# Early shares of an output projection: whole blocks at the heads' ends, or halves spread over more heads

## The chip, the core and the metric

The kernel runs on one core of a Trainium2 chip. The metric is the device time of one execution in microseconds. TensorE (PE in the profile, PEld for its weight loads) does the matmuls, VectorE (DVE), ScalarE (ACT) and GpSimd (POOL) the elementwise work; SyncE (SP) issues the DMA transfers. Each engine takes its instructions in order and waits on semaphores for the others. Matmul results land in PSUM, which the kernel divides into eight buffers of 512 columns.

## What is computed

One inference step of a two-layer decoder over 256 prompt tokens and 64 sample tokens (8 sequences of 8), T = 320 in all, model width 1024. Layer A is a chunked spatial-gating mixer with an FFN behind it; layer B is an mLSTM mixer with 8 heads and again an FFN. The change lies in layer B's mixer:

```
def mlstm_mixer(x, conv_buf, C0, n0, m0, w_in, conv_w, conv_b, b_i, b_f, gn_g, w_out):
    p = x @ w_in
    ...
    qk, new_buf = causal_dwconv(qk_pre, conv_buf, conv_w, conv_b)
    qk = jax.nn.silu(qk).astype(jnp.float32)
    ...
    h, C, n, m = mlstm_chunkwise(q, k, v32, ig, lf, ...)
    ...
    hn = ((h - mu) * lax.rsqrt(var + EPS)).reshape(bsz, s, D_B) * gn_g.astype(jnp.float32)
    o = jax.nn.sigmoid(o_pre.astype(jnp.float32))
    y = (o * hn).astype(x.dtype) @ w_out
    return y, new_buf, C, n, m
```

Each head gives 256 columns of `o * hn`, so the product with `w_out` sums over 8 heads × 256 = 2048 terms, which are 16 slices of 128, two a head. Its 1024 output columns are 8 output blocks of 128. The result is added to the residual stream `x`.

## The kernel before

**Arithmetic.** Everything is float32. A product of accuracy near float32 is made of three matmuls in a faster, rounded format: each operand is split into a high part (rounded) and a low part (the rest), and high × high, high × low and low × high are summed (three matmuls of 128 × 128 weights with 320 columns for each slice of 128). In layer B's mixer (`low_last`) a chunk first runs all matmuls with the weights' high part (the high sweep, two a slice), then all with the low part (the low sweep, one a slice).

**Weights.** `weights` (line 65) writes down the whole order in which weight chunks are used, as a list of (tensor, output block, first slice, slices). A chunk has up to 8 slices. `prefetch` (line 120) loads chunks in that order by SP into `raw` (4 buffers) and splits them: ACT casts the high part `wh` (line 154), DVE subtracts for the low part `wl` (line 155), 3 buffers each. `take` (line 165) hands over the next chunk, and has loads issued 4 chunks and splits 1 chunk ahead. `chunk` (line 173) issues a chunk's matmuls; `block` (line 185) takes a PSUM buffer from the pool `psm` (tag `pm`, 3 buffers) and sums as many chunks as its slices need. A second pool, `psa` (tag `pa`, 5 buffers), serves the smaller sums of the mixer.

**Order.** All matmuls keep the order of the program (`pin`, line 43), and the chunks' casts and subtractions keep theirs among each other. The other DVE and ACT work is put in order by a scheduler, so the program's text alone does not give it.

**A head of layer B** (loop in `layer_b`, from line 1055). For head h (from 1 on) the core runs, in this order on PE: the q block; parts of the state product of head h−1 (`inter`); the k block; the rest of `inter` and the sums of head h−1 (`numer`, tiles `num`); the first v block; the prompt's state (`state_prompt`, tile `pCp`) and a quarter of the samples' state (`state_sample`, tile `pcs`); the second v block; another quarter; `scores` (tiles `pMb`, `psc`); the first output-gate block; a quarter; the second gate block; `finish(h-1)`, which transposes the normalised rows `hn` (tiles `phn`), multiplies by the gate and splits the result into `yhb` and `ylb`, slices 2(h−1) and 2(h−1)+1 for the output projection; the last quarter; `k_nat` and `v_nat` (transposes into `pk`, `pv`, with DVE and ACT work that makes `kgs`, `kgh`, `kgl`, `vh`, `vl`, `vb`); and the first part of `inter` for head h. Six blocks of 8 slices a head are 144 large matmuls. The epilogues (`qk_epi`, `v_epi`, `o_epi`, `stats`) are DVE and ACT work beside that. In heads whose `state_sample` is wide (below h = 6) one of its two tiles comes from `psm`.

**Early output.** Once heads 0 to 3 are finished, their 8 slices can be multiplied with `w_out` before the remaining heads are done. `EARLY_OUT` (line 118) says where: the key (h, r) is a place in head h (r = 0 behind the q block, 1 behind `numer`, 2 ahead of the second v block, 3 behind `scores`, 4 ahead of the second gate block, 5 at the head's end), the value the output blocks whose share of slices 0 to 7 is made there. `early` (line 1015) runs the block and adds it to the residual stream by `residual` (line 301, one DVE add of 128 × 320 out of PSUM, tile `xT`). The other 8 slices follow in and behind head 7: `begin` (line 1048) starts output blocks 0 and 1 in head 7 and block 2 behind it and holds their `psm` buffers until the last heads' slices are added.

**The end of the mixer** (lines 1117 to 1150). Behind head 7 come `begin(0)`, `begin(1)`, the last `inter` and `numer`, the first gate block of head 7, `stats` with the first gate's epilogue in between, `state_prompt`, the second gate block with `o_epi` (line 1136), `finish(7)`, and the output blocks' second halves.

Of the kernel before, what the change touches and what calls it, by code (L numbers as in the profile page):

```python
# [10 lines left out]
F32 = mybir.dt.float32  # L11
# [5 lines left out]
P = 128  # L17
# [5 lines left out]
KD = D // P  # L23
# [14 lines left out]
class Net:  # L38
# [26 lines left out]
    def weights(self):  # L65

        I = self.I
        q = []

        def add(w, b, *groups, k0=0):  # L70
            for kn in groups:
                q.append((w, b, k0, kn))
                k0 += kn


        add(I["a_wv"], 0, 4)
        add(I["a_wv"], 4, 4)
        add(I["a_wv"], 0, 4, k0=4)
        for b in range(1, 4):
            add(I["a_wv"], b, 4, 4)  # L80
        add(I["a_wv"], 4, 4, k0=4)
        for b in range(5, 16):
            add(I["a_wv"], b, 8)
        for b in range(16):
            add(I["a_win"], b, 8)
        for b in range(KD):
            add(I["a_wo"], b, 8, 8)

        def ffn(l):
            for b in range(2 * KF):  # L90
                add(I["f_up"][l], b, 8)
            for b in range(KD):
                add(I["f_dn"][l], b, 8, 7, 7)

        ffn(0)
        add(I["b_wg"], 0, 8)
        for h in range(NH):
            for r in range(6):
                r = (0, 2, 1, 3, 4, 5)[r] if h == 0 else r
                if (h, r) == (NH - 1, 4):  # L100
                    for k0, n in ((8, 4), (12, 2)):
                        for b in (0, 1):
                            add(I["b_wo"], b, n, k0=k0)
                add(I["b_win"], 6 * h + r, 8)
                for b in self.EARLY_OUT.get((h, r), ()):
                    add(I["b_wo"], b, 8)
        add(I["b_wo"], 2, 6, k0=8)
        for b in (0, 1, 2):
            add(I["b_wo"], b, 2, k0=14)
        for b in range(3, KD):  # L110
            add(I["b_wo"], b, 8, k0=8)
        ffn(1)
        self.wq = q
        self.loaded, self.halved, self.used = [], [], 0

    AHEAD, SPLIT_AHEAD = 4, 1
    low_last = False
    EARLY_OUT = {(4, 5): (0, 1), (5, 3): (2,), (5, 5): (3, 4), (6, 3): (5,), (6, 5): (6, 7)}

    def prefetch(self, n, m):  # L120

# [60 lines left out]
                if sweep:  # L182
                    self.mm(ps[:, :T], wl[:, k, :], xh, False, last and k == kn - 1)

    def block(self, kt, rhs):

        ps = self.psm.tile([P, 512], F32, tag="pm", name="pm")
        done = 0
        while done < kt:
            kn = self.wq[self.used][3]  # L190
            self.chunk(ps, lambda k: rhs(done + k), done == 0, done + kn == kt)
            done += kn
        return ps
# [307 lines left out]
    def ffn(self, l, gnext):  # L501
# [3 lines left out]
        with tc.tile_pool(name=f"yf{l}", bufs=1) as yp, tc.tile_pool(name=f"lf{l}", bufs=1) as lp:  # L505
# [58 lines left out]
            else:  # L564
                self.final(lambda m: self.block(KF, rhs), lp)

    def final(self, block, lp):

        nc, O = self.nc, self.O
# [6 lines left out]
        for m in range(last):  # L576
            self.residual(m, block(m))
            self.square_block(m)
            gain(m)

        ps = block(last)
        x = self.xT[:, last, :]
        sq = self.tp.tile([P, T], F32, tag="sq", name="sq", bufs=2)
# [51 lines left out]
    def layer_b(self):  # L635
        nc, tc, I, O = self.nc, self.tc, self.I, self.O
# [4 lines left out]
        with ExitStack() as ctx:  # L641
# [109 lines left out]
            Y = {}  # L751
# [128 lines left out]
            def k_mask(h):  # L880
                _, _, kgs, kgz = S[h]["kg"]
                if h == NH - 1:
                    for b in range(NB):
                        nc.scalar.activation(kgz[:, b, :], kgs[:, b // 4, :].bitcast(F32), AF.Copy, scale=mk[:, b:b + 1])
                    return
                for i in (0, 4):
                    nc.gpsimd.tensor_tensor(kgz[:, i:i + 4, :], kgs[:, i // 4, :].bitcast(F32).unsqueeze(1).to_broadcast([P, 4, P]),
                                            mk[:, i:i + 4].unsqueeze(2).to_broadcast([P, 4, P]), op=MULT)
# [104 lines left out]
            def o_epi(h, j, ps):  # L993
                o = lp.tile([P, T], F32, tag="ob", name="o_b", bufs=1)
                nc.vector.tensor_tensor(o, ps[:, :T], self.rb, op=MULT)  # L995
                th = lp.tile([P, T], F32, tag="tho", name="th_o", bufs=4)
                nc.scalar.activation(th, o, AF.Tanh, scale=0.5)
                S[h].setdefault("o", []).append(th)

            def finish(h):  # L1000
                s = S[h]
                yh = hp.tile([P, 2, T], F32R, tag="yhb", name="yhb", bufs=6)
                yl = hp.tile([P, 2, T], F32R, tag="ylb", name="ylb", bufs=6)
                for e in range(2):
                    pt = self.psa.tile([P, 512], F32, tag="pa", name="phn")
                    for t in range(3):
                        self.tr(pt[:, t * P:(t + 1) * P], hn[:, t, e * P:(e + 1) * P], self.ident)
                    y = self.tp.tile([P, T], F32, tag="yf", name="y_b", bufs=2)
                    nc.vector.scalar_tensor_tensor(y, s["o"][e], 1.0, pt[:, :T], op0=ADD, op1=MULT)
                    g = gnh[:, 2 * h + e:2 * h + e + 1]  # L1010
                    nc.scalar.activation(yh[:, e, :], y, AF.Copy, scale=g)
                    nc.vector.scalar_tensor_tensor(yl[:, e, :], y, g, yh[:, e, :].bitcast(F32), op0=MULT, op1=SUB)
                    Y[2 * h + e] = (yh[:, e, :], yl[:, e, :])

            def early(h, r):
                for m in self.EARLY_OUT.get((h, r), ()):
                    self.residual(m, self.block(8, lambda k: Y[k]))

            with tc.tile_pool(name="rows", bufs=1) as rp:
                gates(rp)  # L1020
# [22 lines left out]
            def blk():  # L1043
                return self.block(KD, self.x_rhs)
# [12 lines left out]
            for h in range(NH):  # L1057
                if h:
                    qk_epi(h, 0, blk())
                    early(h, 0)  # L1060
                    if h == 1:
                        inter(0, 0)
                        state_split(0, 3)
                    inter(h - 1, 1)
                    qk_epi(h, 1, blk())
                    for i in (2, 3):
                        inter(h - 1, i)
                    numer(h - 1)
                    early(h, 1)
                    ps = blk()  # L1070
                    with self.behind_split():
                        stats(h - 1)
                    v_epi(h, 0, ps)
                    v_first(h - 1)
                    state_prompt(h - 1)
                    state_sample(h - 1, 0)
                    early(h, 2)
                    v_epi(h, 1, blk())
# [39 lines left out]
            h = NH - 1  # L1118
# [6 lines left out]
            ps = blk()  # L1125
# [7 lines left out]
            v_first(h)  # L1133
            state_prompt(h)
            k_mask(h)
            o_epi(h, 1, blk())
            finish(h)
            state_sample(h, 0)
            begin(2)
# [1 line left out]
            for m in range(KD):  # L1141
                ps = part.get(m)
                if ps is None:
                    ps = self.block(8, lambda k: Y[8 + k])
# [155 lines left out]
```

## Time and profile before

| | us |
|---|---|
| median of 3 runs | 955.85 |
| lowest and highest run | 955.83, 956.19 |
| the profiled execution | 956.05 |
| its span, first to last instruction | 954.3 |
| layer B's mixer, first block to last output matmul | about 424 to 712 |

The profile is of one execution. "PE L54 MATMUL pm<-xh,wh" is a matmul on PE from line 54, from the tiles xh and wh into pm; the buffer numbers are left out. Blocks on the layer's input read `xh` and `xl`, early output reads `yhb` and `ylb`. A matmul's length in a row is from start to landing; since matmuls overlap, the next one starts well before that, and the distance of two starts is what a matmul costs PE. Rows of the order in time give start, length, instruction, and in brackets the idle time ahead of it.

### The profile page before, as it was taken

The page shows a single profiled execution, that of the slowest core. Times are in us where ns is not written, and L with a number is a line of the kernel's source. Part 1 is how long each engine was busy: PE and PEld are TensorE (multiplying, and loading weights), DVE is VectorE, ACT ScalarE, POOL GpSimd, SP SyncE. Part 2 cuts the span into 40 slices and gives each one's busy share as a digit, 9 for nine tenths or more (in the row PEclk, how much of TensorE's full clock was granted, in tenths as well). Part 3 has the DMA queues.
Part 4 walks back from the last instruction along what each step waited for, and adds up shares of the span by engine and source line. Part 5 has one row for each costly group of instructions (what it writes and reads, how often), then busy time and mean ns, then how long its engine had stood idle before and what let it go on. Part 6 is the DMA issues. An engine that isn't in the chain of part 4 may idle for free.

```text
span 954.3 us, 17131 instructions
## 1 busy us (share of the span) xinstructions
PE 947.3 (99%) x6427; PEld 933.8 (98%) x6427; DVE 697.3 (73%) x1331; ACT 531.9 (56%) x978; POOL 115.8 (12%) x291
## 2 busy tenths in 40 slices
PE   9999999999999999999999999999999999999997
PEld 8889999999999999999999999999999999999997
DVE  6766976577777754559999998788897777775443
ACT  7557543454555443458777876666766445544342
POOL 2200000010000000014333322102102000000000
PEclk9999999999999999999999999999999999999999
DMA  8643346444444465565465655553474444445441
GB/s 270 210 153 133 133 137 198 160 146 147 149 156 155 139 183 147 149 216 175 128 212 175 206 178 196 185 183 118 132 247 148 149 145 154 156 144 155 143 141 56
DMA packets 54214, 155.19 MB, mean 163 GB/s; under 512 B 7372, under 2 KB 11980, under 8 KB 54132
## 3 DMA queue, kind: packets, MB, share of 16 engines
q1 hardware_dynamic: 54132, 154.10, 50.5%
q8 instruction: 51, 0.84, 0.4%
q14 instruction: 31, 0.25, 0.1%
HBM read 142.10 MB, written 11.97 MB: 161 GB/s over the span
## 4 chain that ended last, share of the span: by engine, by line
PE 94%; DVE 3%; ACT 1%; POOL 1%; DMA 0%; issue 0%; SPq 0%; POOLq 0%
PE pm L54 81%; PE pv_a L54 6%; PE num L54 2%; PE pmix L54 1%; PE pcs L54 1%; PE psc L54 1%; PE phn L57 0%; PE pCp L54 0%; DMA raw<-in_a_wv 0%; PE pv L57 0%; DVE wl L155 0%; PE pc L54 0%; DVE bcv L767 0%; PE pg L54 0%; PE pk L57 0%
## 5 line engine op out<-in xcount | busy, mean ns | idle before, releaser
L154 ACT CAST wh<-raw 128x1024 fp32r<-128x1024 f32 (+3 forms) x256 | 257.0, 1004 | 294.1 <-PE pm L54 161.7
L155 DVE TENSOR_TENSOR wl<-raw,wh 128x1024 fp32r<-128x1024 f32 (+3 forms) x256 | 299.0, 1169 | 118.9 <-ACT wh L154 115.0
L54 PE MATMUL pm<-xh,wh 128*128 128x320 f32 x1216 | 372.3, 311 | 0.1
L54 PE MATMUL pm<-xl,wh 128*128 128x320 f32 x1216 | 370.3, 309 | 0.0
L54 PE MATMUL pm<-xh,wl 128*128 128x320 f32 x1216 | 321.2, 309 | 0.0
L54 PEld LDWEIGHTS pm<-xh,wh 128*128 128x128 f32 x1216 | 228.4, 188 | 0.4 <-DVE o_b L995 0.3
L54 PEld LDWEIGHTS pm<-xl,wh 128*128 128x128 f32 x1216 | 228.4, 188 | 0.2
L54 PEld LDWEIGHTS pm<-xh,wl 128*128 128x128 f32 x1216 | 214.5, 188 | 0.0
L54 PE MATMUL pm<-yh_f,wh 128*128 128x320 f32 x352 | 108.8, 309 | 0.0
L54 PE MATMUL pm<-yl_f,wh 128*128 128x320 f32 x352 | 108.8, 309 | 0.0
L54 PE MATMUL pm<-yh_f,wl 128*128 128x320 f32 x352 | 108.8, 309 | 0.0
L54 PEld LDWEIGHTS pm<-yh_f,wh 128*128 128x128 f32 x352 | 66.1, 188 | 0.0
L54 PEld LDWEIGHTS pm<-yl_f,wh 128*128 128x128 f32 x352 | 66.1, 188 | 0.0
L54 PEld LDWEIGHTS pm<-yh_f,wl 128*128 128x128 f32 x352 | 66.1, 188 | 0.0
L531 DVE SCALAR_TENSOR_TENSOR fcv<-fpad,vecs,fcv 128x336 f32<-128x336 f32 x88 | 49.6, 565 | 2.1 <-ACT fcv L529 0.7
L54 PE MATMUL pm<-yh_a,wh 128*128 128x320 f32 x128 | 39.6, 310 | 0.0
L54 PE MATMUL pm<-yh_a,wl 128*128 128x320 f32 x128 | 39.5, 309 | 0.0
L54 PE MATMUL pm<-yl_a,wh 128*128 128x320 f32 x128 | 39.5, 309 | 0.0
L533 ACT ACTIVATE fgl<-fcv 128x256 f32<-128x256 f32 x44 | 18.2, 414 | 37.8 <-DVE fcv L531 37.8
L54 PE MATMUL pm<-yhb,wh 128*128 128x320 f32 x128 | 38.1, 311 | 0.0
L54 PE MATMUL pm<-ylb,wh 128*128 128x320 f32 x128 | 37.8, 309 | 0.0
L303 DVE TENSOR_TENSOR xT<-pm,xT 128x320 f32<-128x320 f32 x39 | 19.1, 489 | 25.1 <-PE pm L54 24.9
(286 smaller groups left out, 1371.7 us busy)
## 6 DMA issues: line engine op xcount, KB each, us to landing
raw<-in_f_up SPq DMA_DIRECT2D x88, 512.0 KB, 3.3
raw<-in_b_win SPq DMA_DIRECT2D x48, 512.0 KB, 4.0
raw<-in_f_dn SPq DMA_DIRECT2D x32, 448.0 KB, 3.3
C<-in_C SPq DMA_DIRECT2D x32, 258.0 KB, 3.7
out_Cs<-C SPq DMA_DIRECT2D x32, 258.0 KB, 2.5
raw<-in_a_win SPq DMA_DIRECT2D x16, 512.0 KB, 3.3
raw<-in_a_wo SPq DMA_DIRECT2D x16, 512.0 KB, 4.3
raw<-in_f_dn SPq DMA_DIRECT2D x16, 512.0 KB, 3.5
```

What stands on the lines that cost most here:

```text
L54: self.pin(self.nc.tensor.matmul(out, lhsT, rhs, start=start, stop=stop, skip_group_check=skip))
L154: self.last_split = self.hold(nc.scalar.copy(wh[:, :kn, :], raw[:, :kn, :]))
L155: self.last_low = nc.vector.tensor_tensor(wl[:, :kn, :], raw[:, :kn, :], wh[:, :kn, :].bitcast(F32), op=SUB)
L303: self.nc.vector.tensor_tensor(x, ps[:, :T], x, op=ADD)
L531: nc.vector.scalar_tensor_tensor(cv, pd[:, i:i + NC], self.vec(w + i * KF), cv, op0=MULT, op1=ADD)
L533: nc.scalar.activation(gl[:, :TP], cv[:, :TP], AF.Gelu_apprx_tanh)
```

## The change

Each early share of 8 slices is divided into two of 4 slices, k0 = 0 (heads 0 and 1) and k0 = 4 (heads 2 and 3). Sixteen halves are put at thirteen places from (3, 0) to (6, 5): four in head 3, four in head 4, five in head 5, three in head 6; the first halves of all output blocks lie in heads 3 to 5, the second halves in heads 4 to 6. Before, eight whole shares lay at five places: two at the end of head 4, one behind the scores and two at the end of head 5, the same one and two in head 6. Each half is a weight chunk of its own and ends with a residual add of its own. Besides, the second gate block of the last head takes its PSUM buffer from `psa` in place of `psm`.

```
@@ weights
-                for b in self.EARLY_OUT.get((h, r), ()):
-                    add(I["b_wo"], b, 8)
+                for b, k0 in self.EARLY_OUT.get((h, r), ()):
+                    add(I["b_wo"], b, 4, k0=k0)
...
-    EARLY_OUT = {(4, 5): (0, 1), (5, 3): (2,), (5, 5): (3, 4), (6, 3): (5,), (6, 5): (6, 7)}
+
+    EARLY_OUT = {(3, 0): ((0, 0),), (3, 1): ((1, 0),), (3, 3): ((2, 0),), (3, 5): ((3, 0),),
+                 (4, 1): ((4, 0),), (4, 3): ((5, 0),), (4, 5): ((6, 0), (0, 4)),
+                 (5, 1): ((7, 0),), (5, 3): ((1, 4), (2, 4)), (5, 5): ((3, 4), (4, 4)),
+                 (6, 1): ((5, 4),), (6, 3): ((6, 4),), (6, 5): ((7, 4),)}
...
-    def block(self, kt, rhs):
-
-        ps = self.psm.tile([P, 512], F32, tag="pm", name="pm")
+    def block(self, kt, rhs, ps=None):
+
+        if ps is None:
+            ps = self.psm.tile([P, 512], F32, tag="pm", name="pm")
...
             def early(h, r):
-                for m in self.EARLY_OUT.get((h, r), ()):
-                    self.residual(m, self.block(8, lambda k: Y[k]))
+                for m, k0 in self.EARLY_OUT.get((h, r), ()):
+                    self.residual(m, self.block(4, lambda k: Y[k0 + k]))
...
             k_mask(h)
-            o_epi(h, 1, blk())
+            o_epi(h, 1, self.block(KD, self.x_rhs, self.psa.tile([P, 512], F32, tag="pa", name="pm")))
             finish(h)
```

## The prediction

> **What bounds the kernel now.** I read the page first, then the busy time by stretches of layer B, then the order of single instructions at the two places where the change alters a wait. From the page, busy time by engine and the shares of the chain that ended last:
>
> ```profile
> span 954.3 us, 17131 instructions
> PE 947.3 (99%) x6427; PEld 933.8 (98%) x6427; DVE 697.3 (73%) x1331; ACT 531.9 (56%) x978; POOL 115.8 (12%) x291
> ...
> PE 94%; DVE 3%; ACT 1%; POOL 1%; DMA 0%; issue 0%; SPq 0%; POOLq 0%
> ```
>
> The matmul engine sets the time. Its matmuls overlap, so 99% busy could still hide waits of a tenth of a microsecond; what counts is how often one starts. The windows view gives that: stretch, its length, then busy time (and count) of PE, PEld, DVE, ACT, POOL, the granted clock, DMA share and GB/s. The first row lies in the first FFN; the other two are a head of layer B each, from one first output-gate block to the next: the second row without early output, the third with three early blocks.
>
> ```profile
> 200.00:300.00 100.00, 100.00 (x684) 100.00 (x683) 77.56 (x132) 51.40 (x90) 9.55 (x44) 1.00 0.45 150
> 498.30:526.80 28.50, 28.50 (x210) 28.49 (x209) 26.88 (x66) 22.00 (x51) 10.00 (x13) 1.00 0.59 188
> 555.40:594.50 39.10, 39.10 (x281) 39.09 (x281) 34.48 (x80) 26.80 (x63) 8.95 (x17) 1.00 0.57 189
> ```
>
> In the FFN a matmul of 320 columns starts every 100/684 = 0.146 us. A stretch without an early output block takes 28.5 us with 210 matmuls; one with three whole early blocks takes 10.6 us more with 71 recorded (72 issued) matmuls more: 10.6/72 = 0.147 us each. An early block therefore pays the full matmul price where it stands. It fills no hole, and moving it to another head saves nothing by itself. The vector engine is nearly full beside it (26.9 of 28.5 us), so what has to be asked of the move is whether that engine's queue turns late somewhere.
>
> **The change part by part.** *Matmuls.* Eight shares of 24 matmuls become sixteen of 12 (12 × 0.147 = 1.76 us); the count stays. What could cost is a start. The PE order of single matmuls (start, length) shows both kinds:
>
> ```profile
> 568.60 0.31 PE L54 MATMUL pm<-yhb,wh 128*128 128x320 f32 x1
> 568.75 0.31 PE L54 MATMUL pm<-ylb,wh 128*128 128x320 f32 x1
> ```
> ```profile
> 590.93 0.39 PE L54 MATMUL pm<-yhb,wh 128*128 128x320 f32 x1
> 591.17 0.30 PE L54 MATMUL pm<-ylb,wh 128*128 128x320 f32 x1
> ```
>
> A share that follows another share starts for nothing (0.15 us to its second matmul), the one behind the scores loses 0.24 − 0.15 = 0.09 us. Eight more starts are 0 to 8 × 0.09 = 0.7 us; shares behind the scores go from two to four, so I take 2 × 0.09, rounded to **+0.2**.
>
> *Splits and adds.* Groups of the whole run by form (count | total, mean ns):
>
> ```profile
> L155 DVE TENSOR_TENSOR wl<-raw,wh 128x1024 fp32r<-128x1024 f32 x208 | 254.0, 1223 | 85.9 <-ACT wh L154 83.5 <-PE pm L54 1.9
> L154 ACT CAST wh<-raw 128x1024 fp32r<-128x1024 f32 x208 | 217.9, 1047 | 223.1 <-PE pm L54 102.1 <-issue 101.5 <-PE pv_a L54 11.7
> L303 DVE TENSOR_TENSOR xT<-pm,xT 128x320 f32<-128x320 f32 x39 | 19.1, 489 | 25.1 <-PE pm L54 24.9
> L155 DVE TENSOR_TENSOR wl<-raw,wh 128x512 fp32r<-128x512 f32 x10 | 7.0, 701 | 2.8 <-ACT wh L154 1.5 <-PE pv_a L54 1.1
> L154 ACT CAST wh<-raw 128x512 fp32r<-128x512 f32 x10 | 6.2, 621 | 4.7 <-DMA raw<-in_a_wv 1.8 <-PE pm L54 1.5 <-PE pv_a L54 1.1
> ```
>
> Per block DVE gets 2 × 0.70 − 1.22 = 0.18 us of split and a second residual add of 0.49: 8 × 0.67 = 5.4 us in all; ACT 8 × (2 × 0.62 − 1.05) = 1.6 us. All lies beside matmuls: a head with four halves takes 28.5 + 7.0 = 35.5 us of PE and 26.9 + 4 × 1.19 = 31.7 us of DVE (89%), one with five 37.3 and 32.9 (88%), one with three 33.8 and 30.5 (90%), against 94% in the stretch without any. On the mean the cover stays, cost **0**; without it the 5.4 us would be paid.
>
> *Where the cover is thin.* At the end of heads 4 and 5 two shares run back to back and the next head's q block follows. These are DVE, then ACT, then PE around the first of them now:
>
> ```profile
> 569.24 0.48 DVE L303 TENSOR_TENSOR xT<-pm,xT 128x320 f32<-128x320 f32 x1
> 569.64 0.34 DVE L878 SCALAR_TENSOR_TENSOR kgl<-pk,cols,kgh 128x128 fp32r<-128x128 f32 x1
> 569.90 2.35 DVE L155 TENSOR_TENSOR wl<-raw,wh 128x1024 fp32r<-128x1024 f32 x2
> ```
> ```profile
> 566.57 0.37 ACT L869 ACTIVATE kgs<-pk,cols 128x128 fp32r<-128x128 f32 x1
> 567.09 0.48 ACT L843 ACTIVATE vh<-pv,rc 128x256 fp32r<-128x256 f32 x1
> 567.46 0.37 ACT L877 ACTIVATE kgh<-pk,cols 128x128 fp32r<-128x128 f32 x1
> 567.73 1.05 ACT L154 CAST wh<-raw 128x1024 fp32r<-128x1024 f32 x1
> ```
> ```profile
> 565.09 0.31 PE L54 MATMUL pm<-yhb,wh 128*128 128x320 f32 x1
> ```
> ```profile
> 572.12 0.31 PE L54 MATMUL pm<-xh,wh 128*128 128x320 f32 x1
> ...
> 574.47 0.46 PE L54 MATMUL pm<-xh,wl 128*128 128x320 f32 x2
> ```
>
> The low parts (wl) of the q block are made behind the residual of the first share, now 569.90 to 571.12, and the low sweep wants them at 574.47: 3.35 us to spare. After the change two halves take as long as one block (565.09 to 568.60), so the q block starts at 568.60 and its low sweep, 574.47 − 572.12 = 2.35 us in, at 570.95. The residual's place on DVE hardly moves: the same chain of state, k and v work stands ahead of it and is what holds it now (the first share ended at 568.60, its add began at 569.24). In the changed order the split follows it without the kgl between, so it runs from 569.24 + 0.40 = 569.64 to 570.86: 0.09 us to spare. ACT is the danger: its changed order puts the k block's cast (1.05) and one kgh (0.37) ahead of the third vh, on which DVE's last v correction waits, and behind that stand the residual and the split. From 566.94 that gives vh ready at 566.94 + 1.05 + 0.37 + 0.48 = 568.84; DVE, with Cl moved ahead, reaches the correction about then, so the lateness is near zero. Bounds for each place: 0, and 1.42 − 0.09 = 1.33 us if cast and kgh are paid in full. Both estimates land within 0.1 us of need; I take 0.1 each, **+0.2**. Below nothing is excluded, since the q block waits for nothing there now. The single halves at the ends of heads 3 and 6 have the whole q block behind them before their split is wanted.
>
> *Loads.* The rows of the loads (count, KB, us from issue to landing), two issues for a pair of early blocks, and the matmul that first uses them:
>
> ```profile
> raw<-in_b_wo SPq DMA_DIRECT2D x13, 512.0 KB, 4.0
> raw<-in_b_wo SPq DMA_DIRECT2D x2, 256.0 KB, 3.8
> ```
> ```profile
> 577.56 4.84 SPq L127 DMA_DIRECT2D raw<-in_b_wo  x2
> ```
> ```profile
> 604.18 0.30 PE L54 MATMUL pm<-yhb,wh 128*128 128x320 f32 x1
> ```
>
> Eight more loads, each 3.8 us, issued some 26 us ahead of use. Even if halves cut that lead to half it is three times the landing: **0**; if the cover were gone, 3.8 us a time.
>
> The Trainium skill, page "DMA: Bandwidth & Descriptors", section "Bandwidth", says to batch transfers to 1 MiB, and its section "Anatomy of one DMA" gives about 2.0 us a transfer plus its bytes at 436 GB/s. An estimate by that page: two halves are 2 × 2.6 us against 3.2, 16 us more over eight blocks if nothing hid them. By that rule the change is a loss; this trace's 3.8 against 4.0 us agrees that halving saves little, and its 26 us of lead is why I count nothing.
>
> *The last gate block.* Two of the three block buffers are held there by output blocks already begun, so the second gate block waits until DVE has read the first (PE, then DVE):
>
> ```profile
> 683.89 0.28 PE L54 MATMUL pCp<-vh,kgl 128*128 128x258 f32 x1
> 684.22 0.42 PE L54 MATMUL pm<-xh,wh 128*128 128x320 f32 x1
> 684.47 0.31 PE L54 MATMUL pm<-xl,wh 128*128 128x320 f32 x1
> ```
> ```profile
> 683.68 0.48 DVE L995 TENSOR_TENSOR o_b<-pm,rb 128x320 f32<-128x320 f32 x1
> 684.58 0.54 DVE L963 TENSOR_SCALAR hn<-num,mv,sl 128x256 f32<-128x256 f32 x1
> ```
>
> The read ends at 684.16, the block starts at 684.22. Sums matmuls step 0.12 us, so it could start at 684.01; its first step is 0.25 where 0.15 is usual. In the sums' pool the fifth buffer is free: 0.21 + 0.10 = 0.31 us gained at most, 0 if another wait steps in. Next in line are the transposes of hn, whose inputs are ready by about 685.4, over 2 us early, and the rest is driven by PE. I take **−0.3**.
>
> Sum against the profiled execution (956.05 us, 954.3 of span): 956.05 + 0.2 + 0.2 − 0.3 = 956.15. That run stood 0.2 above the median of 955.85, so the forecast is **955.95 us**: no change that can be told.
>
> **The rivals.** *DVE late at the ends of heads 4 and 5* (slower): the full bound at both, 2 × 1.33 in place of 0.2, gives 955.95 + 2.46 = 958.4. For it: the changed ACT order and a margin of 0.09 us. Against: DVE is itself not earlier there. It decides the sign from about 1.0 us of lateness at each place.
>
> *Other small starts vanish* (faster): reshuffled waits could also remove first steps like the one here, 0.20 against 0.12:
>
> ```profile
> 564.53 0.36 PE L54 MATMUL num<-Ch,Qz 128*128 128x258 f32 x1
> 564.73 0.28 PE L54 MATMUL num<-Cl,Qz 128*128 128x258 f32 x1
> 564.85 0.28 PE L54 MATMUL num<-Ch,Qz 128*128 128x258 f32 x1
> ```
>
> Some three a head over five heads at 0.09 are 1.35; with the 0.3, and no cost elsewhere, 955.85 − 1.65 = 954.2. Nothing names them as removed.
>
> *The last gate block gains nothing* (the move doesn't do what it says): another wait takes its place, 956.25.
>
> *A load comes late*, one landing of 3.8 us: 959.75. The 26 us of lead speak against it.
>
> **How the numbers follow.** About 0.2% (1.9 us) is what a measurement can tell from no change. Forecast 0.70, gate block without gain 0.13, DVE late 0.10 (a fifth of it in smaller sizes that stay within 1.9 us), small starts gone 0.05 (two fifths of it beyond 1.9 us for what I don't see), a late load 0.02. Slower 0.08 + 0.02 = 0.10, faster 0.02, same 0.88. The range holds forecast and gate case, reaches most of the way to the small starts and halfway to the DVE case: 955.0 to 957.3.
>
> **What would show it.** Right: heads at 28.5 us plus 1.76 per half; the q blocks of heads 5 and 6 start their low sweep 2.35 us after their first matmul; the second gate block's first matmul 0.12 us behind the last of pCp; clock 1.00. Wrong: a gap ahead of those low sweeps that ends with wl on DVE, a cast that waits for a load, or a wait of the transposes for a buffer.

## The result, and the profile after

| | before | after |
|---|---|---|
| median, us | 955.87 (955.79 to 956.45, 9 runs) | 958.77 (958.24 to 959.05, 9 runs) |
| ratio | | 1.0027, 95% interval 1.0018 to 1.0035 |
| profiled execution, its span | 956.05, 954.3 | 958.24, 956.5 |

The change makes the kernel 2.9 us slower (0.27%; the interval lies clear of 1); the forecast was 955.95, with 957.3 as the top of the range. First the page of the kernel after, busy time by engine and the shares of the chain that ended last:

```profile
span 956.5 us, 17181 instructions
PE 947.9 (99%) x6427; PEld 933.4 (98%) x6427; DVE 702.3 (73%) x1347; ACT 532.3 (56%) x986; POOL 120.5 (13%) x291
...
PE 91%; DVE 5%; ACT 1%; POOL 1%; issue 1%; DMA 0%; SPq 0%; DVEq 0%; POOLq 0%
```

DVE's 5.0 us more (697.3 to 702.3) look like the 5.4 that were forecast, but the groups show something else in them. One group that the change does not touch has grown by 2.0 us (groups overlap at their ends, so what they gain does not add up to the page's 5.0), before and then after:

```profile
L902 DVE TENSOR_TENSOR Cl<-C,Ch 128x516 fp32r<-128x516 f32 x32 | 21.9, 698 | 0.0
```
```profile
L907 DVE TENSOR_TENSOR Cl<-C,Ch 128x516 fp32r<-128x516 f32 x32 | 23.9, 765 | 0.2
```

The chain has moved from PE (94 to 91%) to DVE (3 to 5%). To find the places, the mixer is cut at the starts of `pMb`, one in each head's scores. Rows of the single instructions, of the kernel before and then after: scores of heads 2 and 7, and the last matmuls.

```profile
497.39 0.34 PE L54 MATMUL pMb<-X,sel 128*128 128x392 f32 x1
...
668.23 0.35 PE L54 MATMUL pMb<-X,sel 128*128 128x392 f32 x1
...
948.84 0.33 PE L54 MATMUL pb<-ident,rcf 128*128 128x64 f32 x2
```
```profile
497.06 0.34 PE L54 MATMUL pMb<-X,sel 128*128 128x392 f32 x1
...
669.47 0.35 PE L54 MATMUL pMb<-X,sel 128*128 128x392 f32 x1
...
951.02 0.33 PE L54 MATMUL pb<-ident,rcf 128*128 128x64 f32 x2
```

From head 2's scores to the last matmul it takes 451.45 us before and 453.96 after: 2.5 us more, and that cut leaves out what lies ahead, in which whole profiles differ (head 2's scores come between 496.95 and 498.18 us in the traces of this study). By stretches from scores to scores, worked out from the same rows (the number of halves that a stretch of the kernel after holds stands behind its time; a whole block is two):

| stretch | before | after | free of waits |
|---|---|---|---|
| head 2 to 3 | 28.53 | 32.05 (2) | 28.53 + 2 × 1.76 = 32.05 |
| head 3 to 4 | 28.55 | 33.83 (3) | 33.81 |
| head 4 to 5 | 35.57 (4) | 36.36 (4) | 35.57 |
| head 5 to 6 | 39.09 (6) | 38.11 (5) | 37.33 |
| head 6 to 7 | 39.11 (6) | 32.06 (2) | 32.05 |
| head 7 to the end | 280.61 | 281.55 | |

Three stretches lose: 0.8 us, 0.8 us, and 0.9 behind the scores of head 7, where the gate block should have gained 0.3. The rest pays 1.76 a half, to 0.02. The end of head 4 and the q block of head 5 behind it in three views of the kernel after, DVE, then GpSimd, then PE:

```profile
577.69 0.49 DVE L851 SCALAR_TENSOR_TENSOR vh<-pv,rc,vh 64x256 fp32r<-64x256 f32 x1
578.21 1.30 DVE L907 TENSOR_TENSOR Cl<-C,Ch 128x516 fp32r<-128x516 f32 x1
579.54 0.35 DVE L883 SCALAR_TENSOR_TENSOR kgl<-pk,cols,kgh 128x128 fp32r<-128x128 f32 x1
579.81 0.47 DVE L851 SCALAR_TENSOR_TENSOR vl<-pv,rc,vh 128x256 fp32r<-128x256 f32 x1
580.20 0.48 DVE L308 TENSOR_TENSOR xT<-pm,xT 128x320 f32<-128x320 f32 x1
580.60 1.22 DVE L159 TENSOR_TENSOR wl<-raw,wh 128x1024 fp32r<-128x1024 f32 x1
```
```profile
576.92 2.04 POOL L892 TENSOR_TENSOR kgz<-kgs,mk 128x512 fp32r<-128x512 f32 x2 [9.81 <-DVE kgs L875]
```
```profile
578.84 0.31 PE L54 MATMUL pm<-xh,wh 128*128 128x320 f32 x1
...
581.04 0.31 PE L54 MATMUL pm<-xl,wh 128*128 128x320 f32 x1
581.87 0.85 PE L54 MATMUL pm<-xh,wl 128*128 128x320 f32 x4 [0.53 <-DVE wl L159]
```

The low sweep of the q block starts 581.87 − 578.84 = 3.03 us behind its first matmul where 2.35 is due, and loses 0.11 more on its second step: 0.8. It waits for `wl`, as the prediction had it. But what ACT was to make late, DVE's last v correction (the `vl` at 579.81), did not wait: the rows of DVE follow one another without a gap over 0.03 us. What is late is the queue behind Cl, the subtraction for the state's low part, which took 1.30 us. In the kernel before, it took 0.68 at the end of the same head, where the mask product on GpSimd was all but over when it began (DVE, then GpSimd):

```profile
568.64 0.68 DVE L902 TENSOR_TENSOR Cl<-C,Ch 128x516 fp32r<-128x516 f32 x1
```
```profile
566.69 2.04 POOL L887 TENSOR_TENSOR kgz<-kgs,mk 128x512 fp32r<-128x512 f32 x2 [7.54 <-DVE kgs L870]
```

In the kernel after it begins 0.75 us before GpSimd's second mask product `kgz` ends (576.92 + 2.04 = 578.96), and ends 0.55 behind it. The `vh` beside the same product, which reads PSUM (`pv`), keeps its length of 0.49. Four of the 32 rows of Cl take 1.30 in the kernel after, at the ends of heads 3 to 6; in the kernel before none is over 0.78.

In head 7 it is the normalization on other engines that PE waits for. PE, then GpSimd and DVE, of the kernel after; then GpSimd and DVE of the kernel before:

```profile
669.47 0.35 PE L54 MATMUL pMb<-X,sel 128*128 128x392 f32 x1
670.28 0.38 PE L54 MATMUL psc<-qh,kh 128*128 128x256 f32 x1 [0.46 <-ACT hn L970]
```
```profile
668.19 1.23 POOL L958 TENSOR_TENSOR sl<-t,mhalf 128x3 f32<-128x3 f32 x1 [6.18 <-DVE t L956]
```
```profile
668.04 0.67 DVE L159 TENSOR_TENSOR wl<-raw,wh 128x512 fp32r<-128x512 f32 x1
```
```profile
665.29 0.85 POOL L953 TENSOR_TENSOR sl<-t,mhalf 128x3 f32<-128x3 f32 x1 [6.18 <-DVE t L951]
```
```profile
665.13 0.47 DVE L990 SCALAR_TENSOR_TENSOR C<-C,dec,pcs 128x258 f32<-128x258 f32 x1
```

The normalization of head 6 (its scale `sl`) ends 669.42 − 669.47 = 0.05 us ahead of the start of `pMb`; before, 668.23 − 666.14 = 2.09 ahead. Of these 2.04 us, 1.66 are DVE, whose last step ahead of `sl` comes that much nearer to `pMb`; 0.38 are `sl` itself, which takes 1.23 in place of 0.85. It began while a split `wl` ran on DVE, in the kernel before beside an operation on DVE that reads PSUM (`pcs`). The normalized rows `hn` read `num` out of the small sums' pool, and the scores take a buffer of that pool: 0.62 + 0.11 of wait, and smaller ones behind (the largest 0.29), 1.3 in all. The gate block does what was forecast:

```profile
686.43 0.28 PE L54 MATMUL pCp<-vh,kgl 128*128 128x258 f32 x1
686.55 0.31 PE L54 MATMUL pm<-xh,wh 128*128 128x320 f32 x1
```

0.8 + 0.8 + 1.3 − 0.3 = 2.6, to 0.1 the 2.5 us of the cut.

### The profile page after: what moved, and what is told of

The parts are those of the page before. It is cut to its first block, busy times and chain, and to the rows that moved or that the text cites. A ratio compares the mean times of both kernels' runs of the same rounds, so it can differ in the third digit from the quotient of the medians.

```text
span 956.5 us, 17181 instructions
## 1 busy us (share of the span) xinstructions
PE 947.9 (99%) x6427; PEld 933.4 (98%) x6427; DVE 702.3 (73%) x1347; ACT 532.3 (56%) x986; POOL 120.5 (13%) x291
## 4 chain that ended last, share of the span: by engine, by line
PE 91%; DVE 5%; ACT 1%; POOL 1%; issue 1%; DMA 0%; SPq 0%; DVEq 0%; POOLq 0%
PE pm L54 79%; PE pv_a L54 6%; PE num L54 2%; DVE wl L159 1%; PE pmix L54 1%; DVE bcv L772 1%; PE pcs L54 1%; PE psc L54 1%; DVE Cl L907 0%; PE pCp L54 0%; PE pc L54 0%; DVE C L995 0%; ACT yhb L1016 0%; DVE vl L851 0%; PE phn L57 0%
## 5 line engine op out<-in xcount | busy, mean ns | idle before, releaser
L308 DVE TENSOR_TENSOR xT<-pm,xT 128x320 f32<-128x320 f32 x47 | 22.9, 486 | 24.9 <-PE pm L54 24.9
```

The source lines that it names most:

```text
L308: self.nc.vector.tensor_tensor(x, ps[:, :T], x, op=ADD)
```

## The experiments

Two theories stood against each other. One: a mask product on GpSimd holds DVE's Cl (Cl stands until the product is done), and that makes the two q blocks late. The other: DVE is behind at the ends of the heads whatever it runs beside. For head 7 there was a third: the matmul cover at the end of head 6 is gone.

### The two parts of the change, each alone

`e1_sums_pool` is the kernel before with only this edit; `e2_halves_only` is the kernel after without it:

```
-            o_epi(h, 1, blk())
+            o_epi(h, 1, self.block(KD, self.x_rhs, self.psa.tile([P, 512], F32, tag="pa", name="pm")))
```

> The kernel before with only the last gate block moved to the sums' pool; the early output blocks stay whole and where they were. Theory (the gate block's part of the sum was right, the loss lies with the halves): the second gate block's first matmul starts 0.12 us behind the last of pCp instead of 0.33, and the time is 0.3 us below the kernel before, 955.55 us. Rival (the fifth buffer of the sums' pool is missed by others, and the loss comes from there): 1 us or more above the kernel before.

> The changed kernel without the move of the last gate block: halves alone. Theory: the wait ahead of the second gate block is back, 0.32 us above the changed kernel, 959.1 us, and all three waits (0.8 us ahead of the low sweeps of the q blocks of heads 5 and 6, 0.7 in head 7's scores) are there. Rival (the sums' pool is short of a buffer because of the gate block): the wait in head 7's scores is gone, 958.4 or less.

The first: 955.55 us beside 956.33 for the kernel before on the same chip (ratio 0.9994, 0.9985 to 1.0003: not told apart). Head 7 to the end takes 280.24 in place of 280.61, 0.37 us less, and `pm` starts 0.12 behind the last `pCp`, as in the kernel after. The second: 960.00 us (ratio 1.0039, 1.0026 to 1.0052), with the step from the last `pCp` to `pm` much longer than the 0.33 of before:

```profile
686.60 0.28 PE L54 MATMUL pCp<-vh,kgl 128*128 128x258 f32 x1
687.63 0.41 PE L54 MATMUL pm<-xh,wh 128*128 128x320 f32 x1 [0.75 <-DVE o_b L1000]
687.88 0.31 PE L54 MATMUL pm<-xl,wh 128*128 128x320 f32 x1
```

The step is 1.03 us instead of 0.12: beside the halves the move of the gate block is worth 282.60 − 281.55 = 1.05 us, not 0.3, because DVE comes later to read the first gate block. All three other waits are unchanged, so the pool's fifth buffer is not their cause.

### The mask product out of the way

The first try moved only the place of `k_mask` in the order of issue:

```
-                if h < NH - 1:
-                    k_mask(h)
...
                 early(h, 5)
+                if h < NH - 1:
+                    with tc.issue_after(self.cl_made.ins):
+                        k_mask(h)
```

(the other names the q block's `wl`, `self.last_low`, in place of Cl).

> The changed kernel, with the GpSimd mask product kgz issued behind the end of the head's state subtraction Cl instead of beside it; the order on every engine is the same. Theory (the mask holds the subtraction: Cl took 1.30 us in the changed kernel where 0.69 is usual): Cl takes 0.69 us, the low sweeps of the q blocks of heads 5 and 6 lose 0.1 us instead of 0.8, 957.3 us; if the mask holds any subtraction from on-chip memory alone, the split wl that now lies beside it is stretched by up to 1 us in its place, and the time stays near 958.8. Rival (the vector engine is simply behind at the end of a head, the long Cl is not the cause): the low sweeps are still 0.7 to 0.8 late, 958.8.

> The changed kernel, with the GpSimd mask product kgz issued behind the q block's split wl; the order on every engine is the same. Theory (the mask holds the subtraction): Cl takes 0.69 us, the low sweeps of the q blocks of heads 5 and 6 lose at most 0.1 us instead of 0.8, and head 7, whose first work on the vector engine stands behind the same Cl, comes 0.6 us earlier to its normalization, so that the wait of 0.7 us in its scores shrinks to 0.1: 958.8 - 1.4 - 0.6 = 956.8 us. Rival (the vector engine is simply behind): no wait changes, 958.8. Rival for head 7 alone (its lateness comes from the cover that was taken from the end of head 6, 1.7 us): low sweeps on time, the scores still wait, 957.4.

958.83 and 958.52 us (ratios 1.0026 and 1.0023). Neither decides between the theories, because the edit did not do what it was meant to: the order of issue put no wait on GpSimd, which ran the mask where it had run it, beside Cl, and Cl took 1.30 in both. The next two give GpSimd something to wait for:

```
+                    seen = nc.gpsimd.tensor_copy(self.late[0:1, :], S[h]["Cs"][-1][1][0:1, 0, 0:2].bitcast(F32))
+                    with tc.issue_after(seen.ins):
+                        k_mask(h)
```

(the other reads the q block's `wl` instead of Cl).

> The changed kernel; GpSimd now reads two numbers of the head's last state subtraction Cl before its mask product kgz, so that the mask really starts behind Cl (an order of issue alone had left it where it was). Theory (the mask holds the subtraction): Cl takes 0.69 us instead of 1.30. What the mask then lies beside tells how far the hold reaches: if only some subtractions are held, the split wl of the q block takes its usual 1.22 us and the low sweeps of heads 5 and 6 start at most 0.1 us late, 957.4 us or less; if every subtraction from on-chip memory alone is held, wl takes up to 2.2 us and the low sweeps are later than in the changed kernel, 959 to 960. Rival (the vector engine is behind at the end of a head whatever the mask does): low sweeps 0.7 to 0.8 late as before, 958.8.

> The changed kernel; GpSimd reads two numbers of the q block's split wl before its mask product kgz, so that the mask lies behind both Cl and that split. Theory (the mask holds the subtraction): Cl takes 0.69 us, the low sweeps of the q blocks of heads 5 and 6 start at most 0.1 us late instead of 0.8, 957.3 us; head 7's scores come earlier by at most 0.6 us, which would take most of the 0.7 us there as well, 956.7. Rival (the vector engine is simply behind): no wait changes, 958.8. Rival for head 7 (its lateness is the cover taken from the end of head 6, several us, of which Cl is a small part): the low sweeps are on time but the scores still lose over 0.3 us, 957.2.

958.28 us (ratio 1.0023, 1.0014 to 1.0032) and 957.98 (1.0018, 1.0010 to 1.0027): by time neither is told from the kernel after (1.0018 to 1.0035). In the trace the two stretches fall from 36.36 and 38.11 to 35.78 and 37.54 with the mask behind the split, 1.15 us together, and alike with it behind Cl (35.80, 37.57). DVE, GpSimd and PE with the mask behind the split:

```profile
578.90 0.70 DVE L907 TENSOR_TENSOR Cl<-C,Ch 128x516 fp32r<-128x516 f32 x1
...
580.69 1.21 DVE L159 TENSOR_TENSOR wl<-raw,wh 128x1024 fp32r<-128x1024 f32 x1
...
582.48 1.75 DVE L159 TENSOR_TENSOR wl<-raw,wh 128x1024 fp32r<-128x1024 f32 x1
```
```profile
582.11 3.02 POOL L892 TENSOR_TENSOR kgz<-kgs,mk 128x512 fp32r<-128x512 f32 x2
```
```profile
579.53 0.31 PE L54 MATMUL pm<-xh,wh 128*128 128x320 f32 x1
...
581.96 0.85 PE L54 MATMUL pm<-xh,wl 128*128 128x320 f32 x4
```

Cl is back at 0.70 and the low sweep starts 2.43 us in, 0.08 late, where the prediction had 0.09 us to spare and charged 0.1. So the mask beside Cl made most of the lateness, and the rival (no wait changes) falls; with the slow second step each stretch still loses 0.2 in place of 0.8. The hold has not gone away but moved: the mask now lies beside the next `wl`, which takes 1.75 in place of 1.22, and the second mask product waits for that `wl` in turn (3.02 for the pair in place of 2.04). Whichever of the two begins first runs through; the other stands. With the mask right behind Cl this is seen as well (kgz 3.02 beside a `wl` of 1.24 that was already due, the next `wl` 1.40), so the expected choice between "some" and "every subtraction" was put wrongly. Head 7's scores still lose 0.7 in both. That does not clear the hold of it: at the end of head 6 Cl still took 1.30 in the one (the split was made early there, and the mask with it), and in the other the `wl` behind it 1.85.

### One half in place of two ahead of a q block

```
-                 (4, 5): ((6, 0), (0, 4)),
-                 (5, 1): ((7, 0),), (5, 3): ((1, 4), (2, 4)), (5, 5): ((3, 4), (4, 4)),
+                 (4, 5): ((6, 0),),
+                 (5, 0): ((0, 4),), (5, 1): ((7, 0),), (5, 3): ((1, 4), (2, 4)), (5, 5): ((3, 4),), (6, 0): ((4, 4),),
```

> The changed kernel with one half instead of two at the ends of heads 4 and 5; the other half of each pair stands behind the next head's q block. Theory (two halves back to back ask for the q block's split 1.76 us too early for the vector engine): both waits of 0.8 us ahead of the low sweeps go, 957.2 us; head 7's waits stay. Rival (the vector engine is late as such, and the lateness only moves on to the next thing that waits): the same loss at another place of heads 5 and 6, 958.8.

957.14 us (ratio 1.0012, 1.0003 to 1.0020), stretches 35.63 and 37.40, 0.06 and 0.07 above the time free of waits. DVE, then PE at the end of head 4:

```profile
570.93 1.22 DVE L159 TENSOR_TENSOR wl<-raw,wh 128x1024 fp32r<-128x1024 f32 x1
...
578.55 1.30 DVE L907 TENSOR_TENSOR Cl<-C,Ch 128x516 fp32r<-128x516 f32 x1
...
581.34 1.82 DVE L159 TENSOR_TENSOR wl<-raw,wh 128x512 fp32r<-128x512 f32 x2
```
```profile
579.76 1.33 PE L54 MATMUL pm<-xh,wl 128*128 128x320 f32 x8
...
582.11 0.67 PE L54 MATMUL pm<-yhb,wl 128*128 128x320 f32 x3
```

Both waits are gone although Cl still takes 1.30. The q block's split is now made ahead of the work at the head's end (570.93), long before its low sweep (579.76). Behind the held Cl stands the split of the half that follows the q block (581.34 to 582.02), and that one is due only at 582.11. So the 0.8 us need both: a held Cl, and a split due soon behind it.

### Halves where the blocks were

In place of the thirteen places:

```
+    EARLY_OUT = {(4, 5): ((0, 0), (0, 4), (1, 0), (1, 4)), (5, 3): ((2, 0), (2, 4)),
+                 (5, 5): ((3, 0), (3, 4), (4, 0), (4, 4)), (6, 3): ((5, 0), (5, 4)),
+                 (6, 5): ((6, 0), (6, 4), (7, 0), (7, 4))}
```

> The changed kernel's halves and its gate block in the sums' pool, but the halves stay where the whole blocks were (behind the ends of heads 4, 5 and 6 and the scores of heads 5 and 6): dividing without spreading. Theory (dividing is free under the matmuls, the loss comes from where the cover goes): no wait ahead of the low sweeps, none in head 7's scores, 955.6 us. Rival (the 5.4 us of extra splits and adds on the vector engine are what costs): waits as in the changed kernel or more, 958 us and above.

960.09 us (ratio 1.0043, 1.0030 to 1.0055): the theory fell. Each of the three heads' ends loses some 1.44 us (stretches 37.02, 40.52, 40.55). DVE and PE at the first of them:

```profile
567.94 1.30 DVE L906 TENSOR_TENSOR Cl<-C,Ch 128x516 fp32r<-128x516 f32 x1
...
570.33 0.69 DVE L158 TENSOR_TENSOR wl<-raw,wh 128x512 fp32r<-128x512 f32 x1
```
```profile
568.56 0.31 PE L54 MATMUL pm<-yhb,wh 128*128 128x320 f32 x1
...
569.59 0.31 PE L54 MATMUL pm<-ylb,wh 128*128 128x320 f32 x1
571.07 0.73 PE L54 MATMUL pm<-yhb,wl 128*128 128x320 f32 x3 [1.17 <-DVE wl L158]
```

The second half's low sweep follows 1.18 us behind its first matmul and needs a split that stands behind the whole end of the head on DVE. So dividing is not free, and spreading the halves gave part of it back (958.77). But Cl is held here too, with 1.30 us at all three ends, which puts the queue back by some 0.7 us (from Cl to the next operation 579.54 − 578.21 = 1.33 us in the kernel after, 569.24 − 568.64 = 0.60 in the kernel before). By that estimate about half of the 1.44 is the hold, and the rest the shorter time until a split is due; no run has these halves without the hold. In head 7 this kernel takes 280.36 us, 0.1 more than `e1_sums_pool`: with the halves back at the end of head 6, where PE had waited, head 7's waits are gone.

### Head 7

Three kernels on top of `e4_one_half`: a block buffer of the other pool for some state products, one half fewer behind the scores of head 6 and one more behind the q block of head 7, and both.

```
-                wide = h < NH - 2
+                wide = h < NH - 2 or (h == NH - 2 and i < 2)
```
```
-                 (6, 1): ((5, 4),), (6, 3): ((6, 4),), (6, 5): ((7, 4),)}
+                 (6, 1): ((5, 4),), (6, 5): ((6, 4),), (7, 0): ((7, 4),)}
```

> One half instead of two at the ends of heads 4 and 5, as measured at 957.14 us, and in head 7 the first four state products of head 6 use one block buffer of the other pool, as in the heads before; the order on the vector and scalar engines is the same. Theory (the 0.73 us in head 7's scores is a wait for a buffer of the sums' pool which the late normalization still reads): the wait goes, 957.14 - 0.73 = 956.4 us. Rival (the scores wait for the data they multiply, which the vector engine makes late): 957.1.

> One half instead of two at the ends of heads 4 and 5, as measured at 957.14 us, and the half behind the scores of head 6 now stands behind the q block of head 7. Theory (the vector engine comes into head 7 with too little matmul cover behind it; a half brings 1.76 us of matmuls against 1.19 of its own work, 0.57 net, and its work leaves head 6): the scores wait 0.2 us or less instead of 0.73, 956.5 us. Rival (the split of the half comes on top of a vector engine that is already late): the wait grows or another appears ahead of the k block, 957.5 us or more.

> The two edits for head 7 together, on one half at the ends of heads 4 and 5. Theory: no wait of more than 0.15 us is left in heads 2 to 7, 955.8 us, no different from the kernel before with the gate block moved alone (955.55), since a half pays the same matmul price wherever it stands. Rival (halves carry a cost of their own, 0.09 us for each of eight more starts): 956.3 us.

957.19, 957.37 and 957.22 us (ratios 1.0011, 1.0011, 1.0009, all with intervals of ± 0.0009): by time none differs from 957.14, and the runs of each spread over 0.9 to 1.5 us. The traces tell more. With the other pool the scores start at once, and the wait stands one step further on, at the transposes of `hn`, 0.58 us:

```profile
668.58 0.28 PE L54 MATMUL psc<-qh,kh 128*128 128x256 f32 x1
...
669.32 0.65 PE L57 MATMUL phn<-ident,hn 128*128 128x128 f32 x2
670.13 0.66 PE L57 MATMUL phn<-ident,hn 128*128 128x128 f32 x4 [0.15 <-ACT hn L970]
```

So the buffer was only the first thing that a late normalization touched. With the half moved, the last step ahead of `sl` on DVE comes 0.55 us earlier against `pMb` (1.50 ahead became 2.05), about the 0.57 worked out, `sl` takes 0.85 again, and the scores no longer wait; but the second transposes then wait 0.7 us for a buffer:

```profile
670.72 0.55 PE L57 MATMUL phn<-ident,hn 128*128 128x128 f32 x3 [0.55 <-DVE C L995]
```

With both edits neither of these waits is left, and head 7 to the end takes 280.95 in place of 281.56. The expected 955.8 was missed all the same: beside the 280.24 of `e1_sums_pool` 0.7 us remain, in small waits behind the transposes of which the largest (0.29, ahead of a `num` matmul) is over the 0.15 that the theory allowed. What makes these was not found.

The last two kernels have whole blocks, and take one or both of them from the end of head 6, on top of `e1_sums_pool`:

```
-    EARLY_OUT = {(4, 5): (0, 1), (5, 3): (2,), (5, 5): (3, 4), (6, 3): (5,), (6, 5): (6, 7)}
+    EARLY_OUT = {(4, 5): (0, 1), (5, 1): (7,), (5, 3): (2,), (5, 5): (3, 4), (6, 1): (6,), (6, 3): (5,)}
```

> The kernel before with the gate block moved (955.55 us, whole blocks), and one of the two early blocks at the end of head 6 moved behind the k block of that head; nothing is divided. Theory (head 7's waits come from the matmul cover that was taken from the end of head 6, 3.53 us a block against 1.71 us of its own vector work): the vector engine comes 1.8 us later into head 7, and the 1.9 us for which it idled in head 7's q block take that up, so no wait in head 7's scores or normalization, 955.6 us. Rival (only the extra splits of halves make head 7 late): 955.6 as well; this run sets the scale for the next.

> As the one before, with both early blocks of the end of head 6 moved away (one behind the k block of head 6, one behind that of head 5); nothing is divided. Theory: the vector engine comes 3.6 us later into head 7, 1.7 more than its idle time takes up, the normalization's scale sl ends 1.5 us nearer to the end of the last v block, and head 7 shows the changed kernel's waits, 0.7 us at the scores or the transposes and 0.3 to 0.6 behind: 956.5 us. Rival (dividing alone makes head 7 late): no such wait, 955.6 us.

956.03 and 955.74 us (ratios 0.9998, 0.9989 to 1.0007, both). From head 2's scores to the end the first takes 451.08, the very time of `e1_sums_pool`: as expected, DVE's idle time takes it up. The second takes 0.23 more, not the expected 0.9. Its GpSimd and PE rows:

```profile
666.00 1.23 POOL L954 TENSOR_TENSOR sl<-t,mhalf 128x3 f32<-128x3 f32 x1 [6.10 <-DVE t L952]
```
```profile
667.98 0.35 PE L54 MATMUL pMb<-X,sel 128*128 128x392 f32 x1
```

`sl` ends 0.75 us ahead of `pMb`, between the 2.09 of before and the 0.05 of after. The lost cover thus brings 1.34 of the 2.04 us of lateness (0.38 of it again because `sl` takes 1.23), but PE waits mostly for the last part of it, and that part came with the halves. How much of the rest is the held Cl at the end of head 6 and how much the halves' splits was not told apart.

## Why the prediction was wrong

- **Starts of halves, +0.2.** Nothing: 32.05 and 33.83 us are 28.53 plus 1.76 a half, to 0.02. A share behind the scores takes the slow first step (0.23 us) from the gate block that stood there.
- **Splits and adds, 0 because DVE is 88 to 90% busy.** The work came about as forecast (+5.0 of 5.4 us in the groups of `wl` and `xT`), but a mean over a head was the wrong test. With halves in the blocks' places a head's end loses 1.44 us, an estimated half of it by the hold of Cl.
- **Thin cover at the ends of heads 4 and 5, +0.2.** The step that failed; measured 0.8 + 0.8. The place and the wait were right, and the margin was within 0.2 us; "the residual's place on DVE hardly moves" was wrong. DVE's arrival was priced with Cl at its usual 0.68 us, and in the changed order Cl met the mask product and took 1.30. With the hold gone the low sweep is 0.08 us late, with it 0.68. The rival "DVE late at the ends of heads 4 and 5" (958.4) named the place but took ACT's cast and kgh for the cause; ACT's last vh was not what DVE waited for. That its 958.4 comes close to the 958.77 is luck: 1.6 us of the loss stand at its two places, the rest in head 7.
- **Not in the sum: head 7, +1.3.** "The single halves at the ends of heads 3 and 6 have the whole q block behind them" holds for that split; the prediction did not ask what DVE's lateness does some 18 us later. The two blocks' 7 us of matmuls at the end of head 6 had let DVE catch up ahead of head 7, in which the state products take both their tiles from the pool that scores and sums use. Taking these blocks away costs 0.2 us alone; what the halves add to make it 1.3 is not resolved.
- **The last gate block, −0.3.** Right: 0.37 alone. In the changed kernel, where DVE is later, it is worth 1.05.
- **Loads, 0.** Right: no wait of PE in the mixer ends with a transfer. One cast waits 1.53 us for a load (586.44), a sign that the prediction had named, but no matmul waits for that cast. The 16 us that were estimated by the Trainium skill, page "DMA: Bandwidth & Descriptors", section "Anatomy of one DMA — SWDGE (gpsimd) path", for the case that nothing hides the smaller transfers did not come up; the section gives its figures for transfers issued by GpSimd, and these loads are issued by SP.

The hold could have been read before. In head 0 the kernel before shows it, GpSimd and then DVE:

```profile
452.62 1.04 POOL L887 TENSOR_TENSOR kgz<-kgs,mk 128x512 fp32r<-128x512 f32 x1 [0.77 <-ACT Ps L311]
```
```profile
452.91 1.16 DVE L311 TENSOR_TENSOR Pl<-Pf,Ph 128x384 fp32r<-128x384 f32 x1
```

The eight of this subtraction in the kernel before have a mean of 0.63 us; the other seven take 0.54 to 0.56. The version that the runs leave is the kernel before with the gate block moved: 955.55 us, 0.37 us less by its trace, not told from the kernel before by its times.

## What to carry to other kernels

Dividing a block halves the time in which the split of the next piece must be ready, so price the due time of every split behind the divided piece, not the engine's mean load. When a change reorders an engine, look at what each moved instruction will now lie beside on the other engines, and at rows of one operation whose length differs from its group's mean: that can be a wait which the profile shows as work. A wait that is removed by a buffer can come back as the next one in line, as the 0.73 us at head 7's scores came back as 0.58 at the transposes: the late engine was still late.

## What the runs showed of the hardware

A DVE subtraction with both inputs in SBUF (where the kernel's tiles outside PSUM lie) and a GpSimd operation hold each other up, and the one that began first runs through: Cl 1.30 us in place of 0.69 behind a mask product, `wl` 1.75 in place of 1.22, a mask pair 3.02 in place of 2.04 behind a `wl`, and `sl` 1.23 in place of 0.85 behind a `wl`. The profile shows the hold as a longer instruction and not as a wait. DVE operations with an input from PSUM run through beside a product: vh 0.49, and in the run with the mask behind the split the residual add `xT` 0.48 (582.08), which is a TENSOR_TENSOR as Cl is. The Trainium skill, page "SBUF — State Buffer", section "Who interferes with whom", says so: "A DVE instruction with two SBUF inputs contends with a GpSimd instruction that reads SBUF", and "Issue order, not op shape, decides who blocks." These traces agree with it.
